# Reordering the lower-half projection columns and moving seven backward states ahead in an encoder-layer kernel

## The chip, the cores and the metric

The kernel runs on one NeuronCore of a Trainium2 chip. The metric is the device time of one execution in microseconds (us); the kernel before has a median of 3198.08 us over three runs (3193.67 to 3198.31). Five engines matter: PE (TensorE, matrix products; PEld is its weight load), DVE (VectorE), ACT (ScalarE), POOL (GpSimd) and SP (SyncE, which here issues most DMAs). Each engine works through its own list of instructions in order and waits on semaphores where it needs another's result.

## What is computed

One layer of a bidirectional encoder over 2048 tokens of width 1024. A combined projection feeds two groups, a long convolution (Hyena) of order 2 and a matrix-memory recurrence (mLSTM) of 4 heads with 128 features. Their outputs are joined, projected and added to the input; then come cross-attention into 256 memory tokens, a squared-ReLU MLP and a norm.

```python
proj = u @ w_in                       # columns: v, x1, x2 | q, k | value, output gate | 16 gate columns
for o, gate in enumerate((x1, x2)):   # Hyena: FFT convolution over all 2048 tokens, then a gate
    z = gate * (irfft(rfft(z) * spec[:, o]) + z * skip[o])
# mLSTM, forward and with all inputs flipped; per chunk of tokens
num = einsum(s, v) + inter * einsum(q, C)
C_new = carry_decay * C + einsum(we, k, v)
```

The backward direction of the mLSTM needs, for each chunk of 128 tokens, the state `C` that comes from the tokens behind it. With 16 chunks there are 15 such states; state n-1 is made from state n and from the k and value rows of chunk n.

## The kernel before

All matrix products of the projection are done in three passes over high and low halves of the operands (`mm3`, lines 340 to 342), which the page shows as three lines of equal weight. A tile scheduler places the instructions of each engine; what the program hands it is the order in which Python generators are advanced. `weave(a, b, wa, wb)` advances two generators so that their yielded weights keep the ratio wa to wb, `chain` runs generators one after the other, `among(g, h, every)` advances h once for every `every` yields of g, and `take(g, n)` passes on n yields.

The part in question lies between about 340 and 1300 us of the span. In `program` the convolution (`hyena`) is woven with a chain of everything else, at 279 to 499:

- `sweep(cols, hf, ...)` projects columns of the convolution and of q and k for one half of the tokens (hf 0 is the lower half) in tiles of 256 columns: tiles 0 to 3 are v and x1, 4 and 5 are x2, 6 and 7 are q, 8 and 9 are k. Its matmuls are 512 wide. It writes q and k to DRAM (k also transposed, `kn`).
- `natural(hf, tiles)` projects the value columns (tiles 0, 1), the output gate (2, 3) and the gate columns (with tile 3); its matmuls are 256 wide, 24 for each of eight token tiles.
- `gates` computes decays and weights of the recurrence in small steps, mostly on DVE. Five groups of its PE products are pinned in program order.
- `memproj` folds the memory tokens into the attention weights in eight steps: a `project` each, then `keys` for the first four and `values` for the last four. It is also pre-empted by `natural(0, (2,))` before its first `keys`.
- `backward` (lines 1097 to 1109) makes backward states one per yield: load the k and value rows of the chunk (tiles kn and va, line 1064 and 1070), scale the values on POOL (ve, line 1078), eight matmul records for four heads (line 1082, pinned in program order where `far_states` runs it), four DVE operations (line 1088) and a store of the state to DRAM (cbd, line 1107).

The convolution ends, for its second order, with eight steps of the inverse transform (line 177 and 188 on PE, loads at lines 860 and 863, the output to yh at line 955). In the second weave `memproj`'s remaining five steps stand beside the first steps of `mlstm`. `mlstm` loads row factors (tile rows, line 1142), runs `backward` for states of chunks 7 to 1, loads q and k of the first chunks (tiles qn and kk_t, line 1149), and then goes through 16 chunks: scores (line 1175), two kinds of value products (lines 1213 and 1215), a forward state update (again line 1082), and DVE, ACT and POOL work around them. After five chunks `attention` starts (its first matmuls have the tile act, its first transposes are line 1350) and the other eleven chunks are woven with it.

## Time and profile before

| | |
|---|---|
| median of three runs | 3198.08 us (3193.67 to 3198.31) |
| the profiled execution's own time | 3195.44 us |
| its span, first to last instruction | 3193.7 us |
| mean granted TensorE clock | 0.978 |
| PE busy | 3050.3 us, 96% |
| DVE / ACT / POOL busy | 2056.9 (64%) / 1503.6 (47%) / 1156.5 (36%) |
| bytes moved by DMA | 609.48 MB, mean 191 GB/s |

The page gives busy shares of the whole span, then a strip of 40 slices, about 80 us each, that shows where a share is lower. The views by window give the same for any stretch: the busy time of each engine with its number of instructions in brackets, the granted TensorE clock, the DMA engines' busy share and the GB/s. The view of one line gives durations (minimum, median, maximum) and the first and last start. The chain view lists, in order of time, what the last work was waiting on. In the view of SP's own instructions a row is the issue of a DMA, not its transfer.

### The profile page before, as it was taken

Reading aid. Unit: us, or ns where it says so; the run is one execution under the profiler, and the core shown is the slowest. Engines: PE = TensorE matmul, PEld = TensorE weight load, DVE = VectorE, ACT = ScalarE, POOL = GpSimd, SP = SyncE. Lnnn points to the kernel's source line nnn. Section 1 sums busy time; section 2 is a strip of 40 time slices with the busy share of each in tenths; the row PEclk is TensorE's granted clock in tenths of the full one; section 3 lists DMA queues with packets and bytes.
Section 4 is the critical chain, followed back from the end, with each engine's and each line's share of the span. In section 5 each row is a group of like instructions: output and inputs, shape, how many; then the busy total and the mean of one; then the engine's idle time right before and its main releaser. Section 6 shows DMA issues by size and latency. Waiting matters only on the chain.

```text
span 3193.7 us, 43601 instructions
## 1 busy us (share of the span) xinstructions
PE 3050.3 (96%) x14473; PEld 2399.5 (75%) x14473; DVE 2056.9 (64%) x3563; ACT 1503.6 (47%) x2873; POOL 1156.5 (36%) x802
## 2 busy tenths in 40 slices
PE   6999999999999977999999998999999999999998
PEld 4655566776668766888887886888888878888876
DVE  7775366444874767877775556566655676655695
ACT  5543366424764344454544445556555443333335
POOL 0122012100121334324151217776566483434483
PEclk9999999999999987999999998999999999999999
DMA  5564767686677987556384538656644474444334
GB/s 184 198 207 163 249 194 209 170 272 193 174 230 209 294 268 236 174 164 214 105 298 143 177 118 280 211 196 202 230 154 156 149 249 153 141 132 150 124 93 168
DMA packets 447673, 609.48 MB, mean 191 GB/s; under 512 B 39118, under 2 KB 249166, under 8 KB 446424
## 3 DMA queue, kind: packets, MB, share of 16 engines
q1 hardware_dynamic: 409268, 548.18, 54.0%
q10 hardware_dynamic: 38180, 58.51, 5.5%
q8 instruction: 115, 1.88, 0.3%
q14 instruction: 110, 0.90, 0.1%
HBM read 404.15 MB, written 202.41 MB: 190 GB/s over the span
## 4 chain that ended last, share of the span: by engine, by line
PE 76%; DMA 9%; DVE 7%; issue 3%; ACT 3%; POOL 1%; SPq 1%; ACTq 0%; DVEq 0%; POOLq 0%
PE mm L340 16%; PE mm L342 16%; PE mm L341 16%; PE hy L342 5%; PE hy L340 5%; PE hy L341 5%; PE hy L177 3%; PE hy L876 1%; PE mm L845 1%; PE hy L918 1%; DVE wl L345 1%; DMA xt<-in_x_t_dram 1%; PE hy L1213 1%; PE hy L1215 1%; DMA wn<-in_xa_wq_t_dram 1%
## 5 line engine op out<-in xcount | busy, mean ns | idle before, releaser
L345 DVE TENSOR_TENSOR wl<-wn,wh 128x512 fp32r<-128x512 f32 (+1 forms) x364 | 284.2, 816 | 118.5 <-ACT wh L345 118.2
L1540 DVE TENSOR_TENSOR bl<-wr,bh 128x512 fp32r<-128x512 f32 x213 | 242.1, 1143 | 126.0 <-ACT bh L1539 124.8
L1539 ACT CAST ah<-w 128x512 fp32r<-128x512 f32 x284 | 176.3, 623 | 304.9 <-PE hy L341 159.5
L345 ACT CAST wh<-wn 128x512 fp32r<-128x512 f32 (+1 forms) x364 | 208.1, 618 | 234.7 <-PE mm L342 55.3
L923 POOL TENSOR_TENSOR b<-b,a 128x512 f32<-128x512 f32 x64 | 87.6, 1369 | 583.2 <-ACT b L921 458.8
L340 PE MATMUL mm<-xh,wh 128*128 128x512 f32 x640 | 271.1, 425 | 4.5 <-ACT xh L500 2.3
L341 PE MATMUL mm<-xl,wh 128*128 128x512 f32 x640 | 258.1, 404 | 0.8 <-DVE xl L502 0.6
L342 PE MATMUL mm<-xh,wl 128*128 128x512 f32 x640 | 258.8, 405 | 0.0
L1539 ACT CAST bh<-wr 128x512 fp32r<-128x512 f32 x232 | 143.6, 621 | 235.2 <-PE mm L342 181.8
L1540 DVE TENSOR_TENSOR al<-w,ah 128x512 fp32r<-128x512 f32 x236 | 218.7, 928 | 53.6 <-ACT ah L1539 53.5
L342 PE MATMUL mm<-bh,al 128*128 128x512 f32 x576 | 225.3, 394 | 6.2 <-DVE al L1540 3.3
L340 PE MATMUL mm<-bh,ah 128*128 128x512 f32 x576 | 227.0, 394 | 1.3 <-DVE acc L1697 1.2
L341 PE MATMUL mm<-bl,ah 128*128 128x512 f32 x576 | 226.0, 392 | 0.0
L341 PE MATMUL mm<-act,wh 128*128 128x512 f32 x512 | 200.5, 393 | 0.2 <-DVE act L345 0.2
L342 PE MATMUL mm<-act,wl 128*128 128x512 f32 x512 | 199.3, 391 | 0.1
L340 PE MATMUL mm<-act,wh 128*128 128x512 f32 x512 | 198.2, 393 | 0.1
L340 PE MATMUL hy<-bh,ah 128*128 128x512 f32 x448 | 175.2, 391 | 0.0
L341 PE MATMUL hy<-bl,ah 128*128 128x512 f32 x448 | 174.6, 390 | 0.0
L342 PE MATMUL hy<-bh,al 128*128 128x512 f32 x448 | 174.4, 390 | 0.0
L1389 POOL TENSOR_TENSOR ssum<-ssum,sq 128x512 f32<-128x512 f32 x56 | 82.2, 1467 | 254.5 <-ACT sq L1388 252.6
L340 PEld LDWEIGHTS mm<-xh,wh 128*128 128x128 f32 x640 | 121.8, 190 | 65.6 <-issue 29.7
L341 PEld LDWEIGHTS mm<-xl,wh 128*128 128x128 f32 x640 | 121.4, 190 | 51.6 <-issue 24.2
(378 smaller groups left out, 8487.2 us busy)
## 6 DMA issues: line engine op xcount, KB each, us to landing
wr<-hc SPq DMA_DIRECT2D x224, 256.0 KB
w<-in_ff_w_dram SPq DMA_DIRECT2D x172, 256.0 KB
hc<-wn SPq DMA_DIRECT2D x128, 256.0 KB
wn<-in_w_in_dram SPq DMA_DIRECT2D x100, 256.0 KB
hc<-q SPq DMA_DIRECT2D x96, 256.0 KB
fs<-a SPq DMA_DIRECT2D x32, 512.0 KB
a<-fs SPq DMA_DIRECT2D x64, 256.0 KB
a<-zs SPq DMA_DIRECT2D x64, 256.0 KB
```

Of the source, the lines that this page charges most:

```text
L177: b = self.nc.tensor.matmul(*products[-1], start=True, stop=True)
L340: mm(ps, lh, rh, start=start, stop=False)
L341: mm(ps, lh, rl, start=False, stop=False)
L342: mm(ps, ll, rh, start=False, stop=stop)
L345: both = (self.nc.scalar.copy(hi, src), self.nc.vector.tensor_tensor(lo, src, hi.bitcast(F32), ALU.subtract))
L845: nc.tensor.matmul(pp, dm[:, m], t[:, m], start=True, stop=True)
L876: nc.tensor.matmul(pg, em[:, m], y, start=True, stop=True)
L918: nc.tensor.matmul(pp, dm[:, m], t[:, m], start=True, stop=True)
L923: nc.gpsimd.tensor_tensor(xt, xt, hi[:, m], ALU.mult)
L1389: nc.gpsimd.tensor_tensor(ssum, ssum, sq, ALU.add)
L1539: self.nc.scalar.copy(hi, src)
L1540: eng.tensor_tensor(lo, src, hi.bitcast(F32), ALU.subtract)
```

## The change

Three things change. In the lower half of the tokens the chain's order becomes x2 and k (tiles 4, 5, 8, 9), value columns, q (tiles 6, 7), then the output-gate tile 2, which no longer stands inside `memproj`; `gates` is advanced at every second yield of the first sweep in place of every third. `far_states`, which made eight states, becomes `states`, which makes all fifteen, advanced once for each yield from the value columns on. `mlstm` no longer runs `backward` and no longer reads back state 8; its first weave with `memproj` takes 5 steps in place of 13, at weights 55 and 30.

```diff
-        for i in range(8):
-            mem += ([nat[self.NAT_AT[i]]] if i in self.NAT_AT else []) + first[i + 1:i + 2] + second[i:i + 1]
-        items = tr[:4] * 2 + tr[4:] + [nat[c] for c in (3, 0, 1, 2, 3)] + tr[4:] + nat[:2] + mem
+        for i in range(8):
+            mem += first[i + 1:i + 2] + second[i:i + 1]
+        items = tr[:4] * 2 + tr[4:] + [nat[c] for c in (3, 0, 1, 2, 3)]
+        items += [tr[c] for c in (4, 5, 8, 9)] + nat[:2] + tr[6:8] + nat[2:3] + mem
...
         for i in range(8):
-            if i in self.NAT_AT:
-                yield from self.natural(0, (self.NAT_AT[i],))
             yield 11
...
-    def far_states(self):
+    def states(self):
         with self.tc.tile_pool(name="m_b", bufs=1, side="right") as sb:
-            yield from self.backward(sb, 15, 7, None, self.tc.keep_in_program_order, True)
+            yield from self.backward(sb, 15, 0, None, self.tc.keep_in_program_order, True)
...
             packed_rows.append(t)
-        for _ in self.backward(sb, 7, 0, self.old_state(sb, 8)):
-            yield 3
...
-                            p.natural(0, (3,)), among(p.sweep(range(4, 10), 0, False), p.gates(), 3),
-                            among(chain(p.natural(0, (0, 1), p.prep_mem, 2), take(n, 5)), p.far_states(), 1)),
+                            p.natural(0, (3,)), among(p.sweep((4, 5, 8, 9), 0, False), p.gates(), 2),
+                            among(chain(p.natural(0, (0, 1)), p.sweep((6, 7), 0, False),
+                                        p.natural(0, (2,), p.prep_mem, 2), take(n, 3)), p.states(), 1)),
                       279, 499)
             m = p.mlstm(ms)
-            weave(n, take(m, 13), 85, 75)
+            weave(n, take(m, 5), 55, 30)
```

The edit makes the file ten lines shorter: line numbers of the changed kernel are up to 3 lower as far as the states, and 9 to 11 lower behind them. Apart from single rows, only the order between the end of `natural(0, (3,))` and the start of `attention` differs.

The first place is SP's queue behind the row factors, at the start of `mlstm`. Before, the read-back of state 8 (cb) and the k and value rows of the seven states stand there, mixed with attention weights (wn) and output-gate rows (og):

```order
L1142 DMA rows0_10007<-rows_6231 32x1x512 x4
L1142 DMA rows1_10012<-rows_6231 32x1x512 x4
L1094 DMA cb_10017<-cbd_8019 128x516
L1064 DMA kn_10019<-kn_77 128x512
L1070 DMA va_10021<-vd_78 128x4x128
L1064 DMA kn_10024<-kn_77 128x512
L1070 DMA va_10026<-vd_78 128x4x128
L369 DMA wn_10484<-in_xa_wo_dram 128x512
L369 DMA wn_10488<-in_xa_wo_dram 128x512
L369 DMA wn_10492<-in_xa_wo_dram 128x512
```

In the changed program SP has q, k, the backward state (cbn) and the values of the first two chunks at this place:

```order
L1133 DMA rows0_10140<-rows_6202 32x1x512 x4
L1133 DMA rows1_10145<-rows_6202 32x1x512 x4
L1138 DMA qn_10150<-qt_75 128x4x128
L1138 DMA kk_t_10151<-kt_76 128x4x128
L1138 DMA cbn_10154<-cbd_7484 128x516
L1067 DMA va_10156<-vd_78 128x4x128
L1138 DMA qn_10165<-qt_75 128x4x128
L1138 DMA kk_t_10166<-kt_76 128x4x128
L1138 DMA cbn_10169<-cbd_7484 128x516
L1067 DMA va_10171<-vd_78 128x4x128
```

The loads of the first chunk (qn, kk_t) stood 40 rows further back before; now nothing stands between them and the row factors.

The second place is PE in the second convolution. In the changed program the products of states (ve, kn) stand there between those of the convolution (L842, L873 and L915, which were L845, L876 and L918) and the q columns (xh, wh); one piece of it:

```order
L842 MATMUL mm<-a,dm 128x512 x2
L340 MATMUL mm<-xh,wh 128x512
L341 MATMUL mm<-xl,wh 128x512
L342 MATMUL mm<-xh,wl 128x512
L340 MATMUL mm<-xh,wh 128x512
L341 MATMUL mm<-xl,wh 128x512
L1079 MATMUL hy<-ve,kn 128x129 x4
L915 MATMUL hy<-a,dm 128x512
L873 MATMUL hy<-b,em 128x512
```

Before, products of the late states stood on PE behind the convolution, between the value products of `memproj` (wh, wl, kt):

```order
L342 MATMUL mm<-wh,kt 128x512
L1082 MATMUL hy<-ve,kn 128x129 x4
L340 MATMUL mm<-wh,kt 128x512 x2
L1082 MATMUL hy<-ve,kn 128x129 x4
L341 MATMUL mm<-wl,kt 128x512
```

Counted over the whole of PE's list: ahead of the first inverse step of the second convolution stood three states and 440 matmuls of 256 columns, and now stand eleven states and 514. Within the inverse steps stood five states and 486, and now stand four and 400; of them 184 were of output-gate tile 2, and now 62. From there to the first score product stood seven states, 226 matmuls of 256 columns and 72 of 512, and now stand no state, 154 and 24. From the first score to the first product of `attention` stood none of 256 and 24 of 512, and now stand 84 and 72. The 512-wide ones ahead of the inverse steps are the same number in both.

More of the change, by code (lines that the diff above doesn't have):

```diff
@@ L383, in stream @@
         yield cur
-    NAT_AT = {0: 2}
     def inproj_open(self, es):
@@ L1089, in update @@
                                                pc[:, 129 * i:129 * i + 129], ALU.mult, ALU.add)
-    def old_state(self, sb, n):
-        t = sb.tile([128, 4, 129], F32, tag="cf", name="cb", bufs=3)
-        cbd = self.dram("cbd", (15, 128, 516))
-        self.nc.sync.dma_start(out=t.rearrange("d h e -> d (h e)"), in_=cbd[n - 1])
-        return t
     def backward(self, sb, first, last, old, pin=None, lean=False):
```

## The prediction

> **What bounds the kernel now.** I began with the page's strip of 40 slices.
>
> ```profile
> PE   6999999999999977999999998999999999999998
> PEclk9999999999999987999999998999999999999999
> ```
>
> PE is at 90% or more in nearly every slice; the one deep place is slices 14 and 15, about 1118 to 1277 us, where the clock falls too. The change works there and just ahead of it, so I cut the stretch into stages by window: second convolution (850 to 1000), its inverse steps, the rest up to the row factors, the seven near states, and the first chunks.
>
> ```profile
> 850.00:900.00 50.00, 50.00 (x184) 33.74 (x183) 32.80 (x55) 39.41 (x62) 11.50 (x9) 1.00 0.73 213
> 950.00:1000.00 50.00, 48.11 (x304) 38.49 (x303) 30.45 (x46) 29.21 (x55) 12.46 (x10) 1.00 0.75 211
> 1030.60:1127.00 96.40, 88.24 (x591) 71.44 (x592) 70.24 (x160) 31.52 (x60) 35.61 (x23) 0.95 0.98 293
> 1127.00:1164.10 37.10, 31.87 (x202) 28.64 (x202) 24.34 (x52) 16.15 (x28) 9.74 (x10) 0.91 0.71 220
> 1164.10:1205.00 40.90, 30.43 (x152) 26.03 (x152) 23.48 (x67) 16.18 (x36) 14.05 (x12) 0.79 0.94 308
> 1205.00:1281.90 76.90, 54.56 (x324) 50.18 (x323) 57.50 (x182) 31.62 (x120) 34.65 (x28) 0.73 0.74 237
> ```
>
> After the window and its length come busy PE, PEld, DVE, ACT and POOL, then clock, DMA share and GB/s. The convolution is bound by PE (50.00 and 48.11 of 50 us) with DMA at 0.73 to 0.75. The inverse steps are bound by DMA: share 0.98. In the stage of the near states PE is busy 30.43 of 40.90 us at a clock of 0.79, and in the chunk stage 54.56 of 76.90 at 0.73 with DVE busiest, 57.50. So work moved from the last two stages into the convolution pays its full PE time there, and may free more than its PE time here. The chain of waits shows why.
>
> ```profile
> 1165.98 5.15 DMA va<-vd
> 1171.20 1.06 POOL ve L1078
> 1172.30 2.10 PE hy L1082 x8
> ...
> 1202.68 5.21 DMA kk_t<-kt
> ```
>
> A near state is a load, a POOL product, eight PE records and a store in turn, and the first chunk's k arrives only behind all seven.
>
> **The change, term by term.** The sum is made against the profiled execution (3195.44 us; its span is 3193.7, so 1.7 lie around it); that is 2.64 below the median of 3198.08. A plus is later.
>
> *Convolution.* By PE's order (the section on the change) eight more states and 74 more matmuls of 256 columns stand ahead of the first inverse step.
>
> ```profile
> 1041.10:1042.00 0.90, 0.90 (x8) 0.83 (x8) 1.00 1.20 327
> 1032.50:1041.10 8.60, 8.60 (x73) 8.54 (x72) 5.29 (x6) 3.53 (x5) 1.90 (x1) 1.00 1.05 311
> ```
>
> The first row is line 1082 alone, one state at full clock: 0.90 us. The second is a stretch of 256-wide matmuls: 8.60 / 73 = 0.118 us each. So 8 x 0.90 + 74 x 0.118 = 7.2 + 8.7 = **+15.9**. PE is full there, so nothing hides it. A state's POOL product (1.06 us in the chain above) and its DVE work lie beside PE: POOL is busy 11.50 of 50, DVE 32.80. Without that cover a state would also cost PE a wait, which is the rival below. The six pieces of `gates` come closer together; I cost that at nothing, since PE has products of the projection to do meanwhile. Bounds: the stage in which gates ran lost 3.84 us of PE,
>
> ```profile
> 800.00:850.00 50.00, 46.16 (x172) 30.98 (x173) 45.18 (x146) 32.81 (x51) 9.18 (x6) 1.00 0.63 179
> ```
>
> with DVE at 45.18, so from -3.84 to +3.84. The new column order costs nothing itself: the same products and stores, in a stage bound by PE.
>
> SP is the queue where states stand ahead of loads of the convolution. There each row of k or values waits for a buffer that a state's PE product frees, and each store for DVE. In the changed order the convolution's own loads behind such a row are used one or more convolution steps later, so I take no wait.
>
> *Inverse steps.* Fewer bytes fall in this DMA-bound stage: 122 fewer matmuls of the output-gate tile at 24 a token tile are five stores of 128 KB, and SP's order has six fewer weight pieces of 256 KB there, 0.66 + 1.57 = 2.23 MB.
>
> ```profile
> DMA packets 19023, 31.95 MB, mean 290 GB/s; under 512 B 1759, under 2 KB 11999, under 8 KB 19013
> ```
>
> At the 290 GB/s of 1020 to 1130 us that is 2.23 / 0.290 = **-7.7**. Bounds: 0 if the steps' own latencies set the pace, -11.0 if PE does (86 fewer matmuls at 0.118 and one state). The DMA row is the nearest. The last inverse product, now at 1126.4,
>
> ```profile
> L177 PE MATMUL hy<-a,e x32: 592/593/1116, 1030.6 to 1126.4; 128*64 128x512 f32 x32
> ```
>
> is then 8.2 us later, near 1134.6, and with it yh and the buffers that `mlstm` takes over.
>
> *The near states' stage.* SP's own rows:
>
> ```profile
> 1155.63 8.18 SPq L1142 DMA_DIRECT2D rows<-rows  x8
> 1165.11 0.35 SPq L1094 DMA_DIRECT2D cb<-cbd  x1
> ...
> 1200.87 0.43 SPq L1149 DMA_DIRECT2D qn<-qt  x1
> ```
>
> The row factors are issued until 1155.63 + 8.18 = 1163.81, and the first chunk's q at 1200.87. Now they follow directly: 1200.87 - 1163.81 = **-37.1** for the start of the first chunk. What is late next is the q and k transfer itself (5.21 us above), the same as before. Bounds: this cannot be more, for the row factors still come first; it is less if weights of `memproj` are late and stop something that chunks need, down to the seven states' PE time of 7 x 0.90 = 6.3, which is -6.3.
>
> *The chunk stage.* What `memproj` did beside the near states now falls beside the chunks: 84 matmuls of 256 columns and 48 more of 512. DVE is busiest there, so I add the DVE share of the stage that is removed, line 345 alone:
>
> ```profile
> 1164.10:1205.00 40.90, 9.46 (x14) 8.47 (x14) 0.79 0.94 308
> ```
>
> DVE 9.46 us, one for one: **+9.5**. Bounds: 0 if it fits into the 76.90 - 57.50 = 19.4 us in which DVE is idle, and +29.2 if PE keeps its share. For that, a 512-wide matmul is
>
> ```profile
> 776.80:787.90 11.10, 11.07 (x49) 9.17 (x50) 6.71 (x14) 4.90 (x9) 0.00 (x0) 1.00 0.87 253
> ```
>
> 11.07 / 49 = 0.226 us; 84 x 0.118 + 48 x 0.226 = 20.7, and (54.56 + 20.7) / (54.56 / 76.90) = 106.1, 29.2 more than 76.90. I take the DVE row, as DVE's share of the stage (0.75) is the highest of any compute engine.
>
> Sum: 15.9 - 7.7 - 37.1 + 9.5 = -19.4; 3195.44 - 19.4 = 3176.0, and on the scale of the median 3198.08 - 19.4 = **3178.7**. From the first products of `attention` on, both programs are the same, PE is full, and I add nothing.
>
> **Rivals.**
>
> *The chunk stage takes it all in.* DVE's idle 19.4 us hold the 9.46, and PE's filling keeps the clock up, which shortens the chunks' own products: eight records of line 1082 take 2.10 us at 1172.30 and 0.90 at full clock. For it: PE idles 22.3 us there at a clock of 0.73. Against it: a chunk's wait is mostly for DVE and POOL. Time: the sum without +9.5 is -28.9, 3169.2. The Trainium skill, "TensorE: Matmul & The Clock Gate", Part 1, says that PE goes to half clock after an idle window of about 3.4 us and back after a busy one, so denser work there would itself bring the clock back; the stage's 0.73 agrees with that, and what it would do here is this rival.
>
> *No change.* PE keeps its low share in the chunk stage because products of `memproj` and of chunks wait for each other in one list: +29.2 in place of +9.5 makes 15.9 - 7.7 - 37.1 + 29.2 = +0.3, 3198.4. For it: the share was 0.71 with little of `memproj` left. Against it: its products need no chunk.
>
> *Slower: pinned states stop the convolution.* A state's products are pinned on PE, so a late POOL product or value row stops PE with the whole convolution behind it. One such stop is on record:
>
> ```profile
> PE hy L1082 <- POOL ve L1078: 8.2, 1, 8.2
> ```
>
> That is the first near state, where `va` landed late at a DMA share of 0.94. With eleven states in the convolution, the turning point is 19.4 / 8.2 = 2.4 stops; at three it is +5.2 (3203.3, still within what can be told from no change), at five +21.6, and I give five, 3219.7, as its time. For it: the DMA share of 0.73 to 0.75 rises there with eight states' loads. Against it: the eight states ahead of 1127, most of them in the DMA-bound steps, cost PE 1.4 us together:
>
> ```profile
> L1082 PE MATMUL hy<-ve,kn x64: 271/274/422, 979.1 to 1114.2; 128*128 128x129 f32 x64
> ...
>   issue: 1.4, 6
> ```
>
> The Trainium skill speaks against the change here: by the same page, Part 3, "What overlaps and what doesn't", matmuls start and end in program order without exception, so nothing overtakes a state that waits. The 8.2 us agree; by the rule alone each stop would be paid in full, as the turning point has it.
>
> That the states might not really move is settled by PE's order: eleven stand ahead of the inverse steps.
>
> **How the numbers follow.** Forecast 0.55, taken in 0.17, no change 0.13, slower 0.15. About 0.2%, 6.4 us, is what a measurement of this kernel can tell from no change, so faster ends at 3191.7 and slower begins at 3204.5. The forecast (its own range about 3171 to 3191, from gates' +-3.84 and half of the chunk stage's bounds) and "taken in" are faster: 0.72; the third rival is the same: 0.13; the last is slower: 0.15. The range runs from 3165, which is "taken in" with the inverse steps at -11.0 (3165.9), to 3204, which holds no change and three stops. Left out are the 0.15 above, in which the -6.3 end of the near states' stage lies too (15.9 - 7.7 - 6.3 + 9.5 = +11.4, 3209.5), and about 0.04 below.
>
> **What will show it.** Right: line 177 from about 1046 to 1135; in the convolution PE near 50 of 50; row factors and first q directly after each other on SP; the first score near 1177; the first act product near 1260; the chunk stage about 86 us. Wrong: PE waiting at the states' products for ve in the convolution (slower); a chunk stage over 100 us, with PE waiting for weights or for DVE (no change); the q load long behind the row factors, which would make the -37.1 too large; and inverse steps that do not shorten.

## The result and the profile after

The changed kernel has a median of 3190.86 us against 3196.6 of the kernel before on the same chips: a ratio of 0.9983, with a 95% interval of 0.9974 to 0.9992, which is 5.5 us less (2.6 to 8.3). On another chip it was 0.9984 (0.9975 to 0.9994). So it is faster, as forecast, but by 5.5 us and not by 19.4. The forecast's own limit for telling a change from none was 6.4 us, and 5.5 lies inside it; only the 22 executions of each kernel make it clear. One of the changed kernel's took 6005.52 us and is not in the ratio. The profiled execution of the changed kernel took 3194.24 us, with a span of 3192.5 us.

I cut the profile at records of PE that both programs have: the last inverse product of the first order, the first and the last of the second order (lines 177 and 188), the first score, the first act product. The rows by window hold the stage and its length, then busy PE, PEld, DVE, ACT and POOL, clock, DMA share and GB/s. The kernel before with these cuts:

```profile
763.01:1030.59 267.58, 258.09 (x1209) 186.49 (x1205) 178.70 (x357) 165.02 (x273) 48.49 (x36) 1.00 0.68 199
1030.59:1126.36 95.77, 87.61 (x589) 71.33 (x590) 69.82 (x159) 31.18 (x60) 34.97 (x23) 0.95 0.98 295
1126.36:1205.41 79.05, 62.98 (x359) 54.81 (x355) 48.24 (x120) 33.09 (x66) 24.75 (x22) 0.85 0.83 265
1205.41:1278.52 73.11, 51.13 (x296) 47.14 (x296) 54.55 (x178) 30.03 (x117) 34.33 (x27) 0.72 0.72 234
```

The changed kernel:

```profile
765.74:1058.56 292.82, 280.62 (x1346) 205.00 (x1343) 183.16 (x392) 166.06 (x277) 54.96 (x44) 0.98 0.73 206
1058.56:1155.10 96.54, 81.08 (x496) 64.77 (x496) 70.13 (x162) 28.30 (x54) 34.89 (x22) 0.88 0.90 269
1155.10:1196.33 41.23, 28.19 (x183) 24.99 (x179) 25.75 (x59) 20.46 (x42) 15.48 (x14) 0.88 0.74 234
1196.33:1279.31 82.98, 68.52 (x428) 62.26 (x429) 69.16 (x197) 42.49 (x143) 36.62 (x28) 0.87 0.87 280
```

The strip of the page shows it roughly: slices 13 to 15 of PE, counted from 0, read 9, 7, 7 before, at a clock of 9, 8, 7; now they read 8, 7, 8 at 9, 8, 8:

```profile
PE   6999999999999878999999998999999999999998
PEclk9999999999999988999999999999999999999999
```

The dip is shallower, not gone. The last inverse product was forecast near 1134.6; it starts at 1155.1:

```profile
L177 PE MATMUL hy<-a,e x32: 592/592/1117, 1058.6 to 1155.1; 128*64 128x512 f32 x32
```

By the stages, the third has lost its 37.8 us, but the convolution has grown by 25.2 where 15.9 were forecast, and the inverse steps have not shortened although they hold 93 PE records less. One execution can mislead, so the same kernel was profiled again (run e13_after_again below):

```profile
766.84:1057.19 290.35, 278.94 (x1347) 203.90 (x1343) 183.60 (x392) 166.21 (x277) 54.91 (x44) 0.99 0.73 207
1057.19:1145.34 88.15, 76.11 (x495) 59.65 (x496) 69.67 (x160) 27.86 (x54) 36.19 (x22) 0.94 0.93 291
1145.34:1189.08 43.74, 28.65 (x183) 25.95 (x179) 25.21 (x60) 19.34 (x38) 13.63 (x14) 0.85 0.74 231
1189.08:1277.26 88.18, 70.94 (x428) 64.52 (x428) 69.19 (x196) 43.94 (x147) 37.17 (x28) 0.84 0.81 263
```

The inverse steps now take 88.2 in place of 96.5, and the chunk stage 88.2 in place of 83.0. The three stages behind the convolution (below: the stretch) together take 220.8 in the one and 220.1 in the other (247.9 before): what one of them saves, another gives back. In microseconds, with the last column worked out from the terms on record:

| stage | before | after | after, again | gates at every third yield, twice | forecast |
|---|---|---|---|---|---|
| convolution | 267.6 | 292.8 | 290.3 | 283.7, 284.8 | 283.5 |
| inverse steps | 95.8 | 96.5 | 88.2 | 86.8, 90.8 | 88.1 |
| last inverse product to first score | 79.0 | 41.2 | 43.7 | 44.4, 40.5 | 41.9 |
| first score to first act product | 73.1 | 83.0 | 88.2 | 89.5, 88.3 | 82.6 |
| sum | 515.5 | 513.6 | 510.4 | 504.4, 504.4 | 496.1 |

SP's own rows show the mechanism of the third term as forecast. The row factors are followed by q and k at once:

```profile
1181.23 8.02 SPq L1133 DMA_DIRECT2D rows<-rows  x8
1189.30 0.47 SPq L1138 DMA_DIRECT2D qn<-qt  x1
1190.56 0.37 SPq L1138 DMA_DIRECT2D kk_t<-kt  x1
```

In the convolution the waits of PE (engine, waiting tile and line, releaser; us in total, times, longest) are, for the changed kernel:

```profile
PE mm L741 <- ACT st L203: 2.9, 1, 2.9
PE mm L340 <- DVE st L205: 2.6, 2, 2.1
PE mm L727 <- DVE a L846: 1.3, 1, 1.3
```

Line 741 is a transpose of a k tile, which waits for a buffer (mm) that a copy on ACT (line 203) has to empty. No row names ve: the states do not stop PE. What such a wait does next is seen in two windows:

```profile
889.00:893.00 4.00, 1.14 (x5) 0.31 (x5) 3.96 (x5) 3.32 (x7) 0.88 (x1) 1.00 1.09 233
893.20:896.60 3.40, 3.40 (x8) 1.51 (x5) 3.35 (x6) 2.35 (x4) 1.27 (x1) 0.51 1.10 331
```

PE stands still for 2.86 of the first four microseconds, and in the 3.4 that follow the granted clock is 0.51. The first profile has three such windows in this stage, the second two. Each costs about half of its 3.4 us, so the three cost about 5.1 and the two 3.4.

### The profile page after: what moved, and what is told of

It is laid out like the page before. It is cut to its first block, busy times and chain, and to the rows that moved or that the text cites. A ratio compares the mean times of both kernels' runs of the same rounds, so it can differ in the third digit from the quotient of the medians.

```text
span 3192.5 us, 43584 instructions
## 1 busy us (share of the span) xinstructions
PE 3046.9 (95%) x14473; PEld 2396.8 (75%) x14473; DVE 2044.3 (64%) x3563; ACT 1501.9 (47%) x2873; POOL 1159.3 (36%) x802
## 4 chain that ended last, share of the span: by engine, by line
PE 76%; DMA 10%; DVE 6%; ACT 3%; issue 3%; POOL 1%; SPq 1%; ACTq 0%; DVEq 0%; POOLq 0%
PE mm L340 16%; PE mm L342 16%; PE mm L341 16%; PE hy L342 5%; PE hy L340 5%; PE hy L341 5%; PE hy L177 3%; PE mm L842 1%; PE hy L873 1%; PE hy L915 1%; DVE wl L345 1%; PE hy L1202 1%; PE hy L1204 1%; DMA wn<-in_xa_wq_t_dram 1%; PE hy L1079 1%
## 5 line engine op out<-in xcount | busy, mean ns | idle before, releaser
L345 DVE TENSOR_TENSOR wl<-wn,wh 128x512 fp32r<-128x512 f32 (+1 forms) x364 | 284.8, 818 | 125.9 <-ACT wh L345 125.4
L345 ACT CAST wh<-wn 128x512 fp32r<-128x512 f32 (+1 forms) x364 | 207.9, 619 | 219.6 <-PE mm L342 56.7
L1378 POOL TENSOR_TENSOR ssum<-ssum,sq 128x512 f32<-128x512 f32 x56 | 82.6, 1474 | 252.9 <-ACT sq L1377 252.9
```

The costliest lines, as they stand in the source:

```text
L345: both = (self.nc.scalar.copy(hi, src), self.nc.vector.tensor_tensor(lo, src, hi.bitcast(F32), ALU.subtract))
L1378: nc.gpsimd.tensor_tensor(ssum, ssum, sq, ALU.add)
```

## The experiments

Two questions: what made the convolution 7 to 9 us longer than the work moved into it, and what sets the length of the stages behind it, so that 2.3 MB and 86 products less there brought less than forecast. Code is shown in cuts, with `...` where lines are left out. Theories on the first: the closer **gates**, the new **column order**, or the added **states**. On the second: **bytes**, **PE price** (a product costs its PE time), or the **weight ring**: each 256 KB piece of the attention weights is loaded into one of three staging buffers (wn), split by ACT (wh) and DVE (wl), and only then is its buffer free for the next load. Ratios are to the kernel before on the same chip.

**e1: gates at every third yield, all else as changed.**

```diff
-among(p.sweep((4, 5, 8, 9), 0, False), p.gates(), 2),
+among(p.sweep((4, 5, 8, 9), 0, False), p.gates(), 3),
```

> The changed kernel with the gates advanced at every third yield again in place of every second. The stage of the second sweep and the convolution, up to the first inverse step of the second order, took 263.1 us before and 288.5 after, +25.4 where 15.9 of PE work were moved in. Theory 'density' (the closer gates stall PE and bring the half clock): the stage falls to 279 to 282, the granted clock in it is back at 0.99 or more, and the whole time is 6 to 9 us below the changed kernel's, near 3183. Rival 'column order' (k's transposes ahead of the value columns stall PE): the stage stays at 286 to 290 and the time within 3 us of 3191. Rival 'states' (their POOL, DVE and DMA work slows the convolution): also 286 to 290; the next kernel tells it from the column order.

Measured: the convolution 283.7 us, which is the forecast of 283.5 (the 263.1 and 288.5 of the expectation are the same stage, begun about 4.4 us later); 3187.91 us, ratio 0.9978 (0.9969 to 0.9987). The time is higher than the theory's 3183. Repeated as e18:

> The changed kernel with gates at every third yield once more, on one chip with the two before it. The changed kernel as it is gave a ratio of 0.9983 and 0.9984 to the kernel before, this one 0.9978, though its profile showed 9.2 us less. If the stalls of the gates are in most executions of the changed kernel: the convolution at 282 to 285 again and a ratio of 0.9960 to 0.9975. If not: a convolution of 286 to 291 and a ratio of 0.998 or more.

Measured: 284.8 us, 3188.67, ratio 0.9978 (0.9968 to 0.9987). Its convolution by window, and all waits of PE in it:

```profile
765.79:1050.57 284.78, 274.32 (x1346) 202.49 (x1343) 183.97 (x396) 166.90 (x277) 56.56 (x44) 1.00 0.73 210
```

```profile
PE hy L873 <- DVE b L921: 3.9, 3, 2.0
PE mm L340 <- DVE st L205: 2.2, 2, 1.8
PE mm L340 <- ACT st L203: 0.5, 1, 0.5
PE mm L842 <- DVE st L205: 0.4, 1, 0.4
```

PE is busy 274.3 us at full clock: 258.1 before and 16.2 more, the forecast work. The wait at line 741 is gone, with the states and the column order still in place. So the gates are the cause of the longer convolution, in these profiles 5.5 to 9.1 us. The experiments below bear it out: eight profiles with the second yield and the same work ahead of the inverse steps have a convolution of 287.1 to 292.8 us, five with the third yield 282.8 to 284.8, and in seven of the eight, but in none of the five, PE waits 2.6 to 3.5 us at this transpose for ACT's copy. Of the 8.0 us between 292.8 and 284.8, the windows at half clock are 5.1; e6 and e7 below have the wait at the transpose (2.6 and 3.2 us) but no such window, and a convolution of 288.1 and 287.1.

In the medians the gates are about 1.7 us (0.0005 of the time), with intervals that overlap: not clear of noise. Two things on record lie between. The part of the span outside the four stages is 2678.9 and 2679.2 us in the two profiles of the changed kernel and 2682.7 and 2682.4 in e1 and e18, which takes 3.5 us back; and the profiled executions of the changed kernel were 3.4 and 3.0 us slower than its medians, those of e1 and e18 1.0 and 0.0. Over all kernels the profiled execution lies between 7.2 us below its median and 5.6 above, so a difference of a few us in stage lengths of single profiles is no gain in the time.

**e2: the column order and the closer gates, but only the eight far states made early.** The seven near ones stay in `mlstm`, whose lines for them stay as before. Against the changed kernel:

```diff
...
-    p.natural(0, (2,), p.prep_mem, 2), take(n, 3)), p.states(), 1)),
+    p.natural(0, (2,), p.prep_mem, 2), take(n, 3)), p.far_states(), 1)),
...
-weave(n, take(m, 5), 55, 30)
+weave(n, take(m, 13), 85, 75)
```

> The new column order and the closer gates, but only states 15 to 8 made early and the seven near ones in the mlstm as before. By PE's order 8 states (3 before, 11 after) and 1089 matmuls of 256 columns (1016 before) stand ahead of the first inverse step, so PE's work there is 5 x 0.90 + 73 x 0.118 = 13.1 us more than before. 'Density' and 'column order': the stage takes 284 to 288 us (263.1 + 13.1 + 9.5 = 285.7). 'States': 275 to 278. The inverse steps hold 359 matmuls of 256 columns against 486 before: if PE or DMA bytes set their pace, 96.4 falls to about 80 to 85; if weight loads do, it stays over 92. From the last inverse step to the first score: 79 or more again, since the near states are back. Whole time: 3215 to 3222 with the stage at 286 and no gain in the inverse steps, near 3197 with the stage at 276 and the gain.

Measured: convolution 289.8, inverse steps 77.6, to the first score 82.8, chunks 74.1; 3200.85 us, ratio 1.0023 (1.0014 to 1.0032), between the two times expected. With three states less the convolution still is 9 us over its work (267.6 + 13.1 = 280.7): not the states. With the near states back their stage is back, and the kernel is slower than before: the change's gain comes from moving them. The inverse steps came out below 80, where I expected over 92 if weight loads set the pace; but I had not counted the loads. 24 pieces are split there (29 before, in 95.8), 3.23 us each and 3.30 before, so the ring and the products fit alike.

**e3: all fifteen states early, in the old column order, three per yield at the end.** `mlstm` is that of the changed kernel.

```diff
+def threes(g):
+    for i, v in enumerate(g):
+        if i > 3:
+            next(g, None)
+            next(g, None)
+        yield v
...
-take(n, 5)), p.far_states(), 1)),
+take(n, 5)), threes(p.states()), 1)),
```

> The old column order and gates, but all fifteen states made ahead of the mlstm, three per yield from the output-gate tile on. By PE's order the work ahead of the first inverse step is that of before (3 states, 1016 matmuls of 256 columns), and the inverse steps hold 12 states and 582 matmuls (5 and 486 before). All theories on the convolution: 262 to 266 us. The inverse steps: 96.4 + 7 x 0.90 + 96 x 0.118 = 114 if PE work adds up, 96 to 106 if it falls into the waits for weights that PE has there (8.2 us idle before). Last inverse step to first score: 40 to 44, as after. First score to attention's first product: 77 to 80. Whole time 3170 to 3182, faster than the changed kernel, if the column order or the gates are what cost it; over 3195 if states packed closely stop PE, which would show as PE waiting for ve.

Measured: 267.0, 130.0, 45.5 and 69.2 us; 3194.47 us, ratio 1.0003 (0.9994 to 1.0011). The near stage is gone here too (45.5), but twelve states and 582 products make the inverse steps 34 us longer where their PE work is 17.6: all theories expected 96 to 114. PE waits for ve nowhere in it. What is pushed into the inverse steps is paid there at more than PE's time.

**e5: the kernel before, gates at every second yield.**

```diff
-among(p.sweep(range(4, 10), 0, False), p.gates(), 3),
+among(p.sweep(range(4, 10), 0, False), p.gates(), 2),
```

> The kernel before with one number changed: gates advanced at every second yield in place of every third. PE's work ahead of the first inverse step is that of before. With the third yield restored in the changed kernel the stretch from the last inverse step of the first order to the first of the second fell from 292.8 to 283.7 us, where PE's work alone gives 267.6 + 15.9 = 283.5. Theory 'density': here the same stretch grows from 267.6 to 275 to 278, and the time by 5 to 9 us, to 3200 to 3204. Rival 'density costs only in the new column order' (k's transposes close behind): 267 to 269, and the time within 3 us of before.

Measured: 272.3 us, 4.7 more than before, between the two expectations; 3197.34 us, ratio 1.0013 (1.0003 to 1.0022), which is 4.2 us. By the medians closer gates cost in the old order as well, without states or new columns. The waits that show there are others: the longest is one of 3.2 us (`mm` at line 845, for a load of a<-fs), and 6.8 us from about its end on run at half clock, which alone is about 3.4 of the 4.7. So the number changes the order in which the scheduler puts everything, and not one wait; that this one wait comes from it in every execution is not shown.

**e6: 4.19 MB more; e7: 4.19 MB less.** e6 stores the convolution's output a second time; e7 loads half as many columns per piece, and its split reads them twice.

```diff
 nc.sync.dma_start(out=yh[g, :, js], in_=sq[own[g]])
+nc.scalar.dma_start(out=yh2[g, :, js], in_=sq[own[g]])
```

```diff
-nc.sync.dma_start(out=nat, in_=w[128 * k0:128 * k0 + 128, cs])
+nc.sync.dma_start(out=nat[:, 0:256], in_=w[128 * k0:128 * k0 + 128, c0:c0 + 256])
+two = nat[:, 0:256].unsqueeze(1).broadcast_to([128, 2, 256])
...
```

> The changed kernel, in which the convolution's output is stored a second time, to a tensor that nobody reads: 16 more stores of 256 KB in the inverse steps, issued by ACT, 4.19 MB. Theory 'bytes': from the first inverse step to attention's first product the five kernels profiled besides gave 58.9 to 66.3 MB in 219.6 to 247.9 us, all at 265 to 270 GB/s, so the stretch takes 4.19 / 0.267 = 15.7 us more than the 220.7 of the changed kernel, 234 to 239, and the whole time rises by 12 to 16 to 3203 to 3207. Rival 'latency of the weight chain': the stores wait for nothing and nobody waits for them, so 220 to 225 and a rise of 0 to 4 us.

> The changed kernel, in which each load of a 512-column piece of the wide attention weights reads only 256 columns and uses them twice: half of the columns of those two weights are left out, as many loads, splits and products as before. 32 such loads lie between the first inverse step and attention's first product, so 32 x 128 KB = 4.19 MB less. Theory 'bytes': 220.7 - 15.7 = 205 us, 202 to 209, and the whole time 10 to 16 us below 3191. Rival 'latency of the weight chain' (issue, landing, split, buffer free): the count is the same, so 216 to 221 and 0 to 4 us less. Rival 'PE': 498 + 51 products in the first two parts and the rest in the chunks are the same sum, 219 to 221.

The three stages behind the convolution as one window, in the changed kernel, in e6 and in e7:

```profile
1058.56:1279.31 220.75, 177.79 (x1102) 152.02 (x1103) 165.04 (x417) 91.24 (x238) 86.99 (x63) 0.88 0.86 266
```

```profile
1055.47:1278.91 223.44, 178.63 (x1103) 151.15 (x1103) 166.64 (x418) 90.57 (x238) 85.78 (x63) 0.87 0.90 283
```

```profile
1053.51:1279.92 226.41, 177.73 (x1102) 151.50 (x1102) 169.76 (x417) 91.25 (x237) 85.52 (x63) 0.88 0.78 242
```

More bytes make the stretch 2.7 us longer, not 15.7; with fewer it is 5.7 longer, not 15.7 shorter; the rate moves between 242 and 283 GB/s with them. In e6's inverse steps it is 313 GB/s, so the 295 of the kernel before was no ceiling:

```profile
1055.47:1140.36 84.89, 73.09 (x446) 56.38 (x446) 65.20 (x148) 22.76 (x44) 33.73 (x22) 0.88 0.99 313
```

Bytes alone do not set this stretch. The equal 265 to 270 GB/s of the first kernels, on which I had built the theory, only meant that all of them moved about the same bytes. The times rose to 3196.49 (1.0003, 0.9994 to 1.0012) and 3196.86 (1.0009, 1.0000 to 1.0019). Against the changed kernel's ratio that is about 6 and 8 us more, where bytes had 12 to 16 more and 10 to 16 less, and latency up to 4 more and up to 4 less; e6's profiled execution was 3.8 us faster than its median, so its stretch may show too little. Where the rest lies stays open.

**e8: all states ahead of the inverse steps.** Gates at every third yield, and two states per yield from the q columns on.

```diff
-take(n, 3)), p.states(), 1)),
+take(n, 3)), twos(p.states()), 1)),
...
```

> Gates at every third yield and two states per yield from the q columns on, so that all fifteen states stand ahead of the first inverse step (11 before this) and 1200 matmuls of 256 columns (1090). PE's work in the convolution grows by 4 x 0.90 + 110 x 0.118 = 16.6 us over the 283.7 of the kernel with gates at the third yield: 300. Theory 'bytes': what is moved takes its bytes along, 4 states of 0.79 MB and about 2 MB of weights and stores, some 5 MB or 19 us, out of the stretch that follows, so 220.8 falls to about 202 and the time is 0 to 4 us below that kernel's 3187.9. Rival 'latency': the second stretch stays at 215 or more and the time is 8 us or more above it. Rival 'states stop PE when packed': the convolution takes over 308 with PE waiting for ve.

Measured: convolution 302.6, the rest 212.5; 3196.44 us, ratio 1.0007 (0.9998 to 1.0015). Against e1 and e18, 16.6 us of PE work went into the convolution, which grew by 17.8 to 18.9, and the stretch behind it gave back 7 to 8, where bytes had 19 and latency at most 6: in the convolution work is paid in full, behind it a half. PE waits for ve once in the convolution, 1.2 us.

**e4 and e11: four and two staging buffers.**

```diff
-w1 = self.weights(sb, *self.items[1], kc=2, nbufs=3, pin=True)
-self.wst = self.stream(sb, self.items[2:], w1, kc=2, nbufs=3)
+w1 = self.weights(sb, *self.items[1], kc=2, nbufs=4, pin=True)
+self.wst = self.stream(sb, self.items[2:], w1, kc=2, nbufs=4)
...
-sg = sb.tile([128, 16], F32, tag="sg", name="sg", bufs=2)
+sg = sb.tile([128, 16], F32, tag="sg", name="sg", bufs=1)
```

e4 also takes one of the two buffers of the gate columns (sg), which e11, with `nbufs=2` at the same two places, keeps.

> The changed kernel with four staging buffers for weight pieces (wn) in place of three. In its inverse steps PE idles 15.5 of 97.1 us, mostly for the split of weights. Theory 'weight chain' (load, high part, low part, buffer free again, in turn): PE's waits there for ACT wh and DVE wl, 15.4 us after, fall under 9. By PE's order this program puts 513 matmuls of 256 columns into the inverse steps (400 after) and 1071 ahead of them (1090), so the stage itself may be 97 to 103 with PE at 90% or more, and the chunk stage, from which 84 + 33 products are gone, near 77; whole time 5 to 10 us below the changed kernel's. Rival 'DMA rate': waits for wh stay, the stage grows to 108 to 111 with the work added, and the whole time stays within 3 us of 3191.

> The changed kernel with two staging buffers for weight pieces in place of three. 'Weight ring': a piece took 3.58 us in the inverse steps with three buffers and 2.90 with four; with two 5 us or more, the inverse steps over 115 us and the stretch over 250. 'PE price': 372 products in the inverse steps in place of 400, 93 us or a little more for waits that now show, and the stretch 218 to 230.

Measured: with four, 2.90 us per piece in the inverse steps (35 pieces in 101.6 us; the changed kernel 27 in 96.5, which is 3.58, and 27 in 88.2 again, 3.26), but the stretch is 219.6 us and the time 3194.64, ratio 1.0001 (0.9992 to 1.0010): the scheduler used the room to put eight more pieces and 113 more products there. PE's waits for wh and wl in that stage are 11.4 us (15.4 in the changed kernel), not under 9, and the 5 to 10 us expected did not come. With two, 4.04 us per piece (25 in 101.0 us), the stretch 243.6, 3217.29 us, ratio 1.0067 (1.0053 to 1.0081): a loss far beyond PE price's 218 to 230, though less than the ring's own numbers. So the ring is a limit when it is tightened, and no longer the only one with three buffers. The chain of waits of the changed kernel shows the ring at work behind the inverse steps:

```profile
1158.79 0.70 DVE wl L345
1159.51 3.07 DMA wn<-in_xa_wq_t_dram
1162.60 0.63 ACT wh L345
1163.26 0.33 DVE wl L345
1163.59 5.54 DMA wn<-in_xa_wv_dram
1169.21 0.63 ACT wh L345
```

A load begins where a subtraction ends, takes 3.07 to 5.54 us for the same 256 KB, and ACT's split follows at its landing.

**e9: a third of the attention weights' products left out; e10: a quarter of their loads left out.**

```diff
-self.mm3(p[:, m], wh[:, k, ms], wl[:, k, ms], mt[k // 4][0][:, k % 4], mt[k // 4][1][:, k % 4], k == 0, k == 7)
+x = mt[k // 4][0][:, k % 4]
+self.mm2(p[:, m], (wh[:, k, ms], x), (wl[:, k, ms], x), k == 0, k == 7)
...
```

The products of `keys` and `values` lose a pass in the same way.

```diff
-nat = pool.tile([128, 512], F32, tag="wn", name="wn", bufs=nbufs)
-nc.sync.dma_start(out=nat, in_=w[128 * k0:128 * k0 + 128, cs])
+if c0 == 0:
+    nat = pool.tile([128, 512], F32, tag="wn", name="wn", bufs=nbufs)
+    nc.sync.dma_start(out=nat, in_=w[128 * k0:128 * k0 + 128, cs])
```

> The changed kernel, in which the products of the attention weights leave out one of their three passes: a third of those products, with all loads, splits and stores kept. By PE's order 446 products of 256 columns and 64 of 512 are left from the first inverse step to attention's first product (638 and 96), 22.7 + 7.2 = 29.9 us of PE work less; 134 x 0.118 = 15.8 of it in the inverse steps, 8.7 in the chunk stage. Theory 'PE price' (a product costs its PE time in the inverse steps and among the chunks): inverse steps 96.5 - 15.8 = 81, chunk stage 83.0 - 8.7 = 74, the whole stretch 220.7 falls to 194 to 200. Rival 'weight ring' (three staging buffers, each loaded as soon as it is free, set the pace): as many pieces, so the inverse steps stay at 92 to 97 and the stretch at 213 to 221.

> The changed kernel, in which the second half of each wide row block of the attention weights is not loaded; its splits read the first half's staged piece again. 16 of the 62 loads of the stretch are left out, with all splits, products and stores kept. PE's order now has 502 products in the inverse steps (400) and none of 256 columns among the chunks (84). 'PE price': the same sum, inverse steps 96.5 + 102 x 0.118 = 108.5, chunk stage 66 to 75, the stretch 217 to 226. 'Weight ring': a quarter fewer loads at about 3.5 us each is up to 50 us less; the stretch falls under 200.

e9 by window, inverse steps, chunk stage and the whole stretch:

```profile
1054.55:1137.16 82.61, 66.83 (x362) 46.70 (x362) 65.46 (x154) 25.84 (x49) 34.30 (x22) 0.85 0.97 301
1179.47:1266.67 87.20, 62.49 (x384) 55.71 (x385) 70.80 (x197) 44.30 (x149) 37.05 (x28) 0.82 0.83 266
1054.55:1266.67 212.12, 155.83 (x886) 124.34 (x887) 164.70 (x417) 91.36 (x238) 85.92 (x63) 0.83 0.88 278
```

29.9 us of PE work less make the stretch 8.6 us shorter (8.0 against the second profile), and the chunk stage is as long as with all its products. So a product does not cost its full PE time there: PE price as stated falls. The ring's numbers were missed as well: the inverse steps came to 82.6 and not 92 to 97, so products have some part in them. e10 took 214.6 us, 6.1 less than the changed kernel; neither theory's number. The times: 3187.90 (0.9974, 0.9964 to 0.9985) and 3188.68 (0.9979, 0.9969 to 0.9989).

**e14: no low part of the wide weights.**

```diff
-lo = pool.tile([128, kt, n], F32R, tag="wl", name="wl", bufs=bufs)
+lo = None if n > 512 else pool.tile([128, kt, n], F32R, tag="wl", name="wl", bufs=bufs)
...
-self.split(hi[:, k0, cs], lo[:, k0, cs], nat)
+nc.scalar.copy(hi[:, k0, cs], nat)
...
-return hi, lo
+return hi, hi
```

> The changed kernel, in which the wide attention weights have no low part: the product with it takes the high part again, and 32 of the 62 DVE subtractions (0.69 us each) of the stretch are left out; loads, ACT's part and the number of products stay. Theory 'split chain' (a piece costs its load, its high and its low part in turn, and holds its staging buffer until then): 3.58 us a piece fall to 3.2 to 3.3, the inverse steps to 86 to 91, the chunk stage by about 10 x 0.69 = 7 to 74 to 78, the stretch to 203 to 211. Rival 'PE price': as many products, 217 to 223.

```profile
1185.61:1263.53 77.92, 61.57 (x390) 56.24 (x390) 60.26 (x183) 39.37 (x132) 36.84 (x29) 0.85 0.89 287
1056.13:1263.53 207.40, 168.14 (x1103) 142.63 (x1103) 139.98 (x386) 89.86 (x230) 82.36 (x63) 0.91 0.90 284
```

The chunk stage and the whole stretch: as many products, and 13 us less; 3181.60 us, ratio 0.9965 (0.9951 to 0.9978). It is the lowest time of all, 6.8 us below e13 on the same chip, from work that takes no PE time. So this stretch pays for the making of the low parts, whether by DVE's time (25 us less of it) or by the length of each piece's chain, or because a product waits for wl.

**e16 and e17: the wide low parts on POOL, all or every second; gates at every third yield.**

```diff
-self.split(hi[:, k0, cs], lo[:, k0, cs], nat)
+nc.scalar.copy(hi[:, k0, cs], nat)
+nc.gpsimd.tensor_tensor(lo[:, k0, cs], nat, hi[:, k0, cs].bitcast(F32), ALU.subtract)
```

> Gates at every third yield, and the low parts of the wide attention weights made by POOL in place of DVE: 32 subtractions of 0.69 us leave DVE in the stretch, and each takes 1.3 us or more on POOL (its 128x512 products took 1.27 to 1.61 there). If DVE's own time is what the chunk stage lacks: 89.5 falls by 7 to 10, and the time to 3178 to 3184. If the length of each piece's chain is: 0.6 us a piece longer, 32 pieces over three buffers is 6 us more, the stretch from 220.8 to 225 to 230, and the time 3190 to 3196.

> As the one before with only every second of these subtractions on POOL, 16 of 62. DVE time: 11 us less of it in the stretch, half of it in the chunk stage, 3 to 5 us gained, 3183 to 3186. Chain: 3 us more, near 3190.

e17 keeps every second of these subtractions on DVE.

Measured: the stretch 221.5 and 217.9 (219.6 in e18 beside them), 3188.47 and 3188.85, ratios 0.9981 (0.9972 to 0.9990) and 0.9978 (0.9966 to 0.9990). Neither expectation: taking DVE's time away and making each piece's chain longer cancel, or neither matters by itself. Which of the two e14 had removed to its profit stays open.

**e15: the output-gate tile behind the attention weights' first steps.** Gates at every third yield.

```diff
...
-p.natural(0, (2,), p.prep_mem, 2), take(n, 3)), p.states(), 1)),
+p.mem_ready(), take(n, 3), p.natural(0, (2,))), p.states(), 1)),
```

> Gates at every third yield, and the output-gate tile behind the first three steps of the attention weights in place of ahead of them. It needs 4 weight pieces for 192 products of 256 columns, a step of the attention weights 8 for 96: so pieces move into the convolution, where PE is the bound, and products into the inverse steps, where a piece sets the pace. By PE's order 1021 products and 12 states stand ahead of the inverse steps (1090 and 11), 544 in them (379). Theory 'weight ring': the convolution 283.7 - 69 x 0.118 + 0.9 = 276.5, the chunk stage 78 to 82 with about 10 pieces fewer, the inverse steps under 95 although 165 products more stand there, together with 43 for the stage between some 8 us less than the 504.4 of the kernel with gates at the third yield; the time 3178 to 3184. 'PE price': the inverse steps 86.8 + 165 x 0.118 = 106 or more, no gain over 3187.9.

Measured: convolution 300.3, the stretch 215.1; 3194.92 us, ratio 1.0004 (0.9994 to 1.0014). The second half behaved as the ring said (165 products more in inverse steps of 93.6 us, a chunk stage of 77.6), but the convolution, expected at 276.5, gained a wait of its own:

```profile
PE mm L341 <- DVE mt L345: 17.0, 2, 13.9
```

The memory tokens (mt) were still being scaled and split when their products came up in PE's list; the output-gate tile had hidden that.

**e12: half of the row factors issued by ACT.** Gates at every third yield.

```diff
-nc.sync.dma_start(out=t[32 * q:32 * q + 32], in_=by_half[s])
+(nc.scalar if q % 2 else nc.sync).dma_start(out=t[32 * q:32 * q + 32], in_=by_half[s])
```

> The kernel with gates at every third yield, and half of the eight row-factor loads issued by ACT in place of SP. From the first row factor to the first q SP took 7.2 us there. If that issue stands on the way to the first score, as the removal of the seven states showed for what stood behind it, the stage from the last inverse step to the first score falls from 44.4 to 40 to 42 and the time by 2 to 4 us, to 3184 to 3186. If the first score waits for something else by then, no change: 3186 to 3190.

Measured: 43.0 us to the first score (44.4 and 40.5 without), 3191.90 us, ratio 0.9985 (0.9976 to 0.9994). No gain: SP's issue of the row factors is not what the first score waits for.

**e13: the changed kernel again.**

> The changed kernel as it is, on one chip with the next two. Its first profile gave 292.8 us for the convolution at a clock of 0.98 and 96.5 for the inverse steps at 3.58 us per weight piece, where two variants with the same convolution gave 288.1 and 287.1 at a clock of 1.00 and six variants with three staging buffers took 3.2 to 3.4 us a piece. If the half-clock windows and the slow pieces belong to that one execution: 286 to 289, and 88 to 92 for the inverse steps. If they belong to the kernel: 291 to 294, and 95 to 98. The time 3188 to 3193.

Measured: the rows above; 3188.36 us. The convolution at 290.3 lies between, with two half-clock windows in place of three; the inverse steps at 88.2 belong to the first case. No kernel tried beats the changed one by more than the intervals while doing all of its work; the one with gates at every third yield is level with it. With eight profiles of this convolution between 287.1 and 292.8 the half-clock windows belong to some executions and not to all.

## Why the prediction missed the size

The direction was right, and the mechanism of the main term, the near states. The sum was 14 us too large. Two terms failed: the gates, put at nothing in the convolution, and the price of a weight piece in the chunk stage.

*Convolution, +15.9: too small by 6.9 to 9.3.* The work itself was right: 274.3 us of busy PE in e18, 16.2 more than before. What failed is the sentence that the closer gates cost nothing "since PE has products of the projection to do meanwhile"; +3.84 was its bound. PE had other products, but it takes them in its list's order, and with the gates at every second yield that list has a k transpose ahead of its free buffer. Where a stop of 2 to 3 us was followed by a window at half clock, it cost about 1.7 us more. e1 and e18 show in the profiles that the number 2 is the cause, and e5 by its median; states and column order are cleared by e1, e2 and e18. In the medians this term is about 2 us and not clear of noise. SP's head of line, taken as no wait, showed none in the changed kernel.

*Inverse steps, -7.7.* The two profiles give +0.8 and -7.6, and gates at every third yield -8.9 and -5.0. Where the size was about right, that was luck, for its reason was wrong: e6 ran these steps at 313 GB/s and e7 was no shorter with fewer bytes, so bytes did not bind the stage, though its DMA share is 0.98. The bytes left (269 x 96.54 us is 26.0 MB against 28.3) and took no time along in the first profile. The traces count two pieces fewer there (29 splits and 27), not the six loads that the term took from SP's order.

*Near states, -37.1: right.* -37.8 and -35.3; e2 and e3 show it from both sides.

*Chunk stage, +9.5: too small in three of four.* +9.9, +15.1, and +16.4 and +15.2 in e1 and e18. I priced 14 splits by DVE's time (9.46 / 14 = 0.68 us each). How many pieces each stage split can be read from ACT's row; the chunk stage before, in the changed kernel and in e6:

```profile
L345 ACT CAST wh<-wn x5: 607/618/621, 1209.0 to 1277.4; 128x512 fp32r<-128x512 f32 x5
```

```profile
L345 ACT CAST wh<-wn x20: 607/620/633, 1205.3 to 1279.2; 128x512 fp32r<-128x512 f32 x20
```

```profile
L345 ACT CAST wh<-wn x29: 602/619/628, 1188.9 to 1278.9; 128x512 fp32r<-128x512 f32 x29
```

5 pieces in 73.1 us and 29 in 96.7: (96.7 - 73.1) / 24 = 0.98 us for each piece. That gives 87.8 for 20 pieces; the stage took 83.0 and, with 19 to 21 pieces, 88.2, 89.5 and 88.3, and 87.2 in e9 with a third fewer products. A straight line through the chunk stages of all twenty profiles, counted in the same way, gives 66 us and 1.1 us for each piece, with single kernels up to 7 us off it. So a piece that `memproj` splits beside the chunks costs about 1 us, not 0.68. In most kernels its products come with it; only e9, in one profile, parts the two. In the near states' stage 28 pieces began their split before; now 15 do, and the rest had to go somewhere. The number moved (15 more in the chunk stage) was about right in the sum, and the price of each too low. Why it is 1 us stays open: e14 gained by leaving low parts out, e16 and e17 gained nothing by moving them off DVE. A common step stands behind the terms of the later stages: I charged each stage by its busiest resource, DMA and then DVE, and took the stages as separate. Together they were forecast at -35.3 and measured at -27.2 and -27.9, and the kernels with gates at every third yield have -27.2 and -28.3. With 15.9 + 4.7 for gates (e5) and -27.5 for the rest the sum is -6.9; the medians say -5.5. That e5's 4.7 and the medians' 2 for the gates differ is part of what single profiles leave uncertain.

*Rivals.* "Taken in" was wrong: the clock did come back, 0.72 to 0.87 and 0.84, yet the stage grew. The Trainium skill, "TensorE: Matmul & The Clock Gate", Part 1, would have had denser work speed the chunks up; the clock agrees with it, but the time rose with the pieces. "No change" is the rival whose number came nearest (+0.3 against the -5.5 measured and the -19.4 forecast), but not by its mechanism: it put +29.2 into PE's share of the chunk stage, which grew by 9.9 and 15.1, and in e9 a third fewer products did not shorten it. "Slower" did not occur: eleven states passed the convolution without a wait for ve, and fifteen in e8 with one of 1.2 us.

Open: what the gates cost in a usual execution, between the 2 us of the medians and the 5.5 to 9.1 of the profiles, and whether the length of a piece's chain or DVE's time is what the last stages pay.

## What to carry to other kernels

When work is taken out of a stage that waits, ask what else was hidden in that wait: here a 37 us stage also gave cover to 28 weight pieces, and 9.9 to 15.1 us of the gain went back where some of those pass now. Stages that share one queue of staged pieces should be priced together, by the number of pieces that pass, since a busy share of 0.98 on DMA did not mean that bytes set the pace. And a number that only says how closely a side task is interleaved is an edit of its own: it deserved a term, not a nothing. One profiled execution of such a kernel is not enough: here two of the same program differed by 8 us in one stage and by 5 in another.

## What the runs showed of the hardware

In the changed kernel stops of PE of 2.15 and 2.86 us were each followed by a window of 3.4 us at half clock. They need not be: in e6 and e7 stops of 2.6 and 3.2 us at the same transpose were followed by none, and the number of such windows differs between executions of one program (three, then two). Loads of the same 256 KB took 3.07 and 5.54 us within one short piece of the chain above. The Trainium skill, "DMA: Bandwidth & Descriptors", section "Latency and other measured facts", says that memory access takes much longer under high load than on average; the spread would fit that, but no run here separates load from queueing.
